# A decoder layer in float32 on one core: the second SwiGLU's gate and up blocks in seven half products, all products in 256 columns

## The chip, the core and the metric

One NeuronCore of a Trainium2 chip computes one hybrid decoder layer for 512 tokens. The metric is the time of one execution in microseconds of the device, as the median of several runs. A profiled execution gives the trace from which the rows below are taken; it is a run of its own, with its own time.

## What is computed

Three sub-layers, each with RMSNorm, a shift and a scale before it and a gate on its residual: a half-step SwiGLU, a token mixer (gated convolution and sparse attention), and a second half-step SwiGLU. The model width is 1024, the SwiGLU's inner width 2816.

```
def _swiglu(h, w_gate, w_up, w_down):
    return (jax.nn.silu(h @ w_gate) * (h @ w_up)) @ w_down
...
h = _modulate(_rmsnorm(x, g_ffn1), sh1, sc1)
x = x + MACARON_W * gt1 * _swiglu(h, w1_gate, w1_up, w1_down)
h = _modulate(_rmsnorm(x, g_mix), sh2, sc2)
x = x + gt2 * _hybrid_mixer(h, ...)
h = _modulate(_rmsnorm(x, g_ffn2), sh3, sc3)
x = x + MACARON_W * gt3 * _swiglu(h, w2_gate, w2_up, w2_down)
return _rmsnorm(x, g_final)
```

Everything is float32, and the weights arrive as float32.

## The kernel before

The residual x lies transposed in SBUF: 8 tiles (`DK`) of 128 channels by 512 tokens (`T`). To keep float32 precision at TensorE's float32r rate, every operand is split in two parts, a high one (ScalarE, ACT, copies it to float32r) and a low one (the difference, on VectorE, DVE, or GpSimd, POOL). A product then is three matrix products that add up in one PSUM bank: high x high, low activation x high weight, high activation x low weight. `mm3` issues these three for one chunk of 128 rows of the contraction, each over all columns (tokens) of its output, 512 where nothing else is said, 256 where a half of the tokens is asked for.

Weights come in units of 128 x 1024 values (512 KB) through four raw tiles (`load_unit`, on SP's queue), are split by `make_units` (ACT, line 378) and `low_part` (DVE or POOL, line 367) into one of four pairs of tiles `whi`, `wlo`, and are freed when their products are issued.

A SwiGLU (`ffn`) has 22 blocks of 128 inner columns (`FK`). The first three are made in the stage before, while the norm's halves come in (`first_group`, in halves of 256 tokens; in the first SwiGLU `first_products`, whose last six chunks go over 512). For each further block `project` makes the gate and then the up product, 8 chunks each, into two PSUM banks; `glu` takes the gate's silu (ACT), multiplies by the up product (DVE, line 612) and splits the result into `ghi` and `glo` (ACT, DVE line 619). After 11 blocks comes the first half of the down projection (`part`, 8 output tiles of 11 chunks), whose results are added to x (line 640), and after 22 the second, whose last two output tiles go in halves of 256 tokens, so that the norm behind it can begin (`residual`, line 544, squares on ACT, sums on DVE line 475). Behind the second SwiGLU stands the final norm: `final` scales the first half on DVE (line 1749), `turn` transposes the second and evicts four tiles on ACT or DVE.

The order on each engine is made by a planner while the program is built: `Plan` runs the tasks above, gives each operation a cost by the functions `c_act`, `c_tt`, `c_mm3` and so on, and issues in each step the one that can start first, ties by rank. Where an operation can run on DVE or POOL it takes the one that would end first, with a tax on POOL (`POOL_TAX`). Every engine then executes its list strictly in that order, waiting on semaphores. All products are issued at line 286, so the profile names them by their tiles: `hhi`, `hlo` (the normed input), `ghi`, `glo` (the inner activations), `whi`, `wlo` (weights), `b` (PSUM banks). `whik` is a kept weight tile at a stage's end.

## Time and profile before

| | |
|---|---|
| median of 3 runs | 1047.43 us (1046.82 to 1047.58) |
| the profiled execution | 1046.38 us, of which the span of its instructions is 1044.6 us |
| busy: PE, DVE, ACT, POOL | 1018.8, 608.8, 408.5, 60.2 us |
| granted clock of TensorE, mean over the span | 0.994 of full speed |
| read from HBM | 130.14 MB |

A row of a stretch or group gives the busy time, and how many instructions it holds. A matrix product's busy time reaches from its start to its modelled end, which lies in the next ones' time, since products are pipelined; so the sum of such times is not what a stretch takes, and the distance from one start to the next is the pace. "<-" names what ended an idle time. Stages can be told by the tiles: up to 59 us the first norm and the conditioning, 59 to 386 the first SwiGLU, then its tail and the norm, 410 to 676 the mixer with its output projection, 676 to 706 the second SwiGLU's first three blocks, 706 to 1017 the rest of it, and then the tail.

### The profile page before, as it was taken

To read this page: it belongs to the slowest core of one execution; us is meant where nothing else is said; L and a number is where in the kernel's file an instruction comes from. 1 tells how busy PE (TensorE), PEld (TensorE's weight loads), DVE (VectorE), ACT (ScalarE), POOL (GpSimd) and SP (SyncE) were. 2 spreads that over 40 slices of the span, in tenths; PEclk is the share of its full clock that TensorE was granted. 3 is DMA by queue.
4 is the path that set the end of the run, shared out by engine and by line. 5 is a ranking of instruction groups with operands and counts; after the bars stand their busy time and mean duration, and the time that the engine had idled before them with its cause. 6 is when DMAs were issued, how large, how long until landed. Compare 5 with 4: busy or idle time off the path is not lost.

```text
span 1044.6 us, 13818 instructions
## 1 busy us (share of the span) xinstructions
PE 1018.8 (98%) x5409; PEld 856.6 (82%) x5409; DVE 608.8 (58%) x1065; ACT 408.5 (39%) x719; POOL 60.2 (6%) x51
## 2 busy tenths in 40 slices
PE   7999999999999999998999999999999999999997
PEld 5778888888888889987878778998888888888887
DVE  4987559555555547499898986745333333333334
ACT  4553322222322233347868985334322123222321
POOL 0320000000000002012111110000000000000000
PEclk8999999999999999999999999999999999999999
DMA  9656554554555330433411004133333333333202
GB/s 336 258 214 231 194 202 175 198 201 170 194 201 189 135 106 16 133 113 106 158 39 29 14 20 147 43 103 122 99 101 101 94 91 98 101 101 93 91 19 81
DMA packets 40706, 133.60 MB, mean 128 GB/s; under 512 B 4704, under 2 KB 8032, under 8 KB 40000
## 3 DMA queue, kind: packets, MB, share of 16 engines
q1 hardware_dynamic: 40640, 132.71, 37.4%
q8 instruction: 42, 0.69, 0.2%
q14 instruction: 24, 0.20, 0.1%
HBM read 130.14 MB, written 2.10 MB: 127 GB/s over the span
## 4 chain that ended last, share of the span: by engine, by line
PE 84%; DVE 11%; ACT 2%; issue 1%; DMA 1%; SPq 0%; DVEq 0%; ACTq 0%
PE b L286 82%; DVE PT L1430 1%; DVE wlo L367 1%; DVE afirst L748 1%; DMA wfirst<-in_wa_dram 1%; DVE P L1347 1%; PE b L1419 1%; DVE q L1111 1%; DVE s L531 1%; ACT whi L378 0%; DVE s L1061 0%; ACT P L1351 0%; DVE swp L1064 0%; ACT P L1394 0%; DVE v L401 0%
## 5 line engine op out<-in xcount | busy, mean ns | idle before, releaser
L286 PE MATMUL b<-hhi,whi 128*128 128x512 f32 (+1 forms) x1020 | 380.3, 373 | 1.4 <-DVE pc L1270 1.3
L286 PE MATMUL b<-hlo,whi 128*128 128x512 f32 (+1 forms) x1020 | 375.3, 368 | 0.8 <-DVE hlo L537 0.4
L286 PE MATMUL b<-hhi,wlo 128*128 128x512 f32 (+1 forms) x1020 | 374.9, 368 | 0.0
L378 ACT ACTIVATE whi<-raw 128x1024 fp32r<-128x1024 f32 (+3 forms) x176 | 178.0, 1012 | 452.7 <-PE b L286 310.7
L367 DVE TENSOR_TENSOR wlo<-raw,whi 128x1024 fp32r<-128x1024 f32 (+3 forms) x158 | 186.6, 1182 | 213.1 <-ACT whi L378 211.8
L286 PEld LDWEIGHTS b<-hhi,whi 128*128 128x128 f32 x1020 | 192.8, 189 | 35.7 <-issue 3.9
L286 PEld LDWEIGHTS b<-hhi,wlo 128*128 128x128 f32 x1020 | 192.7, 189 | 31.9
L286 PEld LDWEIGHTS b<-hlo,whi 128*128 128x128 f32 x1020 | 192.9, 189 | 31.2 <-DVE hlo L537 1.3
L286 PE MATMUL b<-ghi,whi 128*128 128x512 f32 (+1 forms) x364 | 136.5, 375 | 0.0
L286 PE MATMUL b<-ghi,wlo 128*128 128x512 f32 (+1 forms) x364 | 135.7, 373 | 0.0
L286 PE MATMUL b<-glo,whi 128*128 128x512 f32 (+1 forms) x364 | 135.7, 373 | 0.0
L612 DVE TENSOR_TENSOR s<-sg,b 128x512 f32<-128x512 f32 x44 | 30.1, 687 | 101.2 <-PE b L286 95.4
L286 PEld LDWEIGHTS b<-ghi,whi 128*128 128x128 f32 x364 | 68.5, 188 | 12.8 <-issue 0.8
L286 PEld LDWEIGHTS b<-ghi,wlo 128*128 128x128 f32 x364 | 68.5, 188 | 12.0
L286 PEld LDWEIGHTS b<-glo,whi 128*128 128x128 f32 x364 | 68.6, 188 | 11.9
L879 DVE SCALAR_TENSOR_TENSOR ada<-araw,cact,ada 128x1024 f32<-128x1024 f32 x49 | 62.8, 1281 | 8.5 <-DMA araw<-in_wa_dram 8.1
L367 POOL TENSOR_TENSOR wlo<-raw,whi 128x1024 fp32r<-128x1024 f32 (+2 forms) x18 | 41.4, 2299 | 258.2 <-ACT whi L378 190.0
L544 DVE SCALAR_TENSOR_TENSOR x<-b,mod,x 128x512 f32<-128x512 f32 (+1 forms) x30 | 19.1, 642 | 38.5 <-PE b L286 38.4
L462 ACT ACTIVATE s<-x 128x256 f32<-128x256 f32 (+1 forms) x41 | 19.5, 491 | 55.1 <-DVE x L544 53.7
L535 ACT ACTIVATE hhi<-s,mod 128x256 fp32r<-128x256 f32 (+1 forms) x42 | 20.9, 534 | 32.4 <-DVE s L531 29.4
L619 DVE TENSOR_TENSOR glo<-s,ghi 128x512 fp32r<-128x512 f32 x44 | 32.2, 736 | 0.0
L1430 DVE TENSOR_TENSOR PT<-b,PT 128x384 fp32r<-128x384 f32 (+1 forms) x48 | 27.9, 594 | 4.0 <-ACT PT L1428 3.9
(241 smaller groups left out, 962.9 us busy)
## 6 DMA issues: line engine op xcount, KB each, us to landing
araw<-in_wa_dram SPq DMA_DIRECT2D x56, 512.0 KB
raw<-in_f1b_dram SPq DMA_DIRECT2D x38, 512.0 KB
raw<-in_f2b_dram SPq DMA_DIRECT2D x38, 512.0 KB
raw<-in_f1d_dram SPq DMA_DIRECT2D x22, 512.0 KB
raw<-in_f2d_dram SPq DMA_DIRECT2D x22, 512.0 KB
raw<-in_wib_dram SPq DMA_DIRECT2D x14, 512.0 KB
wfirst<-in_wa_dram SPq DMA_DIRECT2D x5, 1024.0 KB
raw<-in_wc_dram SPq DMA_DIRECT2D x8, 512.0 KB
```

What stands on the lines that cost most here:

```text
L286: nc.tensor.matmul(o, lhsT, rhs, start=start, stop=stop)
L367: (nc.vector if e == DVE else nc.gpsimd).tensor_sub(wlo_of[j][:, :n], raw_of[i][:, :n], whi_of[j][:, :n].bitcast(F32))
L378: nc.scalar.activation(whi_of[j][:, :n], raw_of[raw_at[u]][:, :n], AF.Copy)
L462: nc.scalar.activation(o[:, ts], x[d][:, ts], AF.Square)
L531: nc.vector.scalar_tensor_tensor(t, x[d][:, ts], am[:, s, d:d + 1], rb(), op0=OP.mult, op1=OP.mult)
L535: nc.scalar.activation(hhi[d][:, ts], t, AF.Identity, bias=sh)
L544: nc.vector.scalar_tensor_tensor(x[d][:, ts], bank_of[b][:, ts], gate, x[d][:, ts], op0=OP.mult, op1=OP.add)
L612: nc.vector.tensor_mul(scr_of[q], sg_of[k], bank_of[bu])
L619: nc.vector.tensor_sub(glo[j], scr_of[q], ghi[j].bitcast(F32))
L748: nc.vector.scalar_tensor_tensor(a[:, 0], w[:, k], cact[:, k:k + 1], a[:, 0], op0=OP.mult, op1=OP.add)
L879: nc.vector.scalar_tensor_tensor(a, w, cact[:, k:k + 1], a, op0=OP.mult, op1=OP.add)
L1430: nc.vector.tensor_sub(pl[:, :w], pt[:, :w], ph[:, :w].bitcast(F32))
```

## The change

Four things change. **(a)** `mm3` splits every output of 512 columns in two pieces of 256 (`HALVES`), and issues its three products for the first and then for the second; four chunks of the first plain gate block of either SwiGLU go in three pieces (`THIRDS`). **(b)** The second SwiGLU is a function of its own, `ffn2`. Blocks 3 to 6 are made as before (in pieces of 256); blocks 7 to 21 by `seven`. There the four quarters of a block's result (gate and up, each for the first and the second half of the tokens, A and B) come from seven products over half of the contraction and half of the tokens, where the plain way takes eight: the 2 x 2 scheme of Strassen and Winograd. Operands of four of the seven are sums. On the weight side `sums` makes them for each block (lines 461 to 472, in the raw tiles) and `sum_parts` splits them (ACT line 479, DVE or POOL line 481) into the tiles `wsh`, `wsl`; on the token side `build_t` makes four sums once (lines 819 to 829, tiles `thi`, `tlo`). `collect` adds the partial results up from two PSUM banks (lines 901 to 926). The even and the odd chunks of the contraction are the two halves; the weights are laid out for it (`KPOS`). **(c)** The down projection goes in four groups of 6, 6, 5 and 5 blocks, each after the first block of the next group. **(d)** The planner's costs are tables, `_MIXER` and `_LATE`, the latter for all after the first stage but the mixer; POOL's tax is 4 in the SwiGLUs. Left out below are the other cost functions, which read the tables, and the layout of the second SwiGLU's weights in HBM.

```
-    def mm3(o, w, x_, start, stop):
-
-        mm(o, w[0], x_[0], start, False)
-        mm(o, w[0], x_[1], False, False)
-        mm(o, w[1], x_[0], False, stop)
+    THIRDS = (slice(0, 176), slice(176, 344), slice(344, T))
+
+    def mm3(o, w, x_, start, stop, pieces=HALVES):
+
+        n = o.shape[-1]
+        if n != T or x_[0].shape[-1] != T:
+            pieces = (slice(0, n),)
+        for ts in pieces:
+            x0, x1 = x_[0][:, ts], x_[1][:, ts]
+            mm(o[:, ts], w[0], x0, start and ts is pieces[0], False)
+            mm(o[:, ts], w[0], x1, False, False)
+            mm(o[:, ts], w[1], x0, False, stop and ts is pieces[-1])
...
+_LATE = dict(act=(0.19, 0.85e-3), tt=(0.16, 1.04e-3), stt=(0.215, 1.04e-3), ts=(0.2, 0.54e-3), ptt=(0.2, 2.5e-3),
+             pts=(0.26, 0.83e-3), mm=0.1133, dma=0.4e-3, small=0.19)
...
 def c_mm3(n):
-    return PE, 3 * max(n / 2370, 0.105)
+    return PE, 3 * _cost["mm"] * max(n / 256, 1)
...
+    def sums(p):
...
+        x = yield scr
+        s1 = scr_of[x]
+        e = yield c_tt(T), (*c_ptt(T), W_TAX)
+        either(e).tensor_add(s1, up[:, E], up[:, O])
+        e = yield c_tt(T), (*c_ptt(T), W_TAX)
+        either(e).tensor_sub(up[:, E], ga[:, E], up[:, E])
+        done(p.third)
+        go(R_W, sum_parts(p, "1", s1, scr, x))
+        yield made[a]
+        e = yield c_tt(T), (*c_ptt(T), W_TAX)
+        either(e).tensor_sub(ga[:, E], s1, ga[:, E])
+        p.freed(scr, x, give)
+        go(R_W, sum_parts(p, "2", ga[:, E], raws, raw_at[a]))
+        e = yield c_tt(T), (*c_ptt(T), W_TAX)
+        either(e).tensor_sub(ga[:, O], ga[:, O], ga[:, E])
+        go(R_W, sum_parts(p, "4", ga[:, O], raws, raw_at[a]))
...
+            def product(o, w, x_, start=False):
+
+                yield PE, DK // 2 * 3 * 0.1133
+                for e in range(DK // 2):
+                    (w0, w1), (x0, x1) = w(e), x_(e)
+                    for i, (u, v) in enumerate(((w0, x0), (w0, x1), (w1, x0))):
+                        nc.tensor.matmul(o, u, v, start=start and not e and not i, stop=e == DK // 2 - 1 and i == 2,
+                                         skip_group_check=not start)
...
+            def collect(by):
+                Y = bank_of[by]
+                q = yield scr
+                v, w = scr_of[q][:, A], scr_of[q][:, B]
+                yield has[1]
+                yield c_act(T // 2)
+                nc.scalar.activation(v, X[:, A], AF.Copy)
+                done(has["copied"])
+                yield has[6]
+                yield c_tt(T // 2)
+                nc.vector.tensor_add(v, v, Y[:, A])
+                yield has[7]
+                yield c_tt(T // 2)
+                nc.vector.tensor_add(w, v, Y[:, B])
+                done(has["w"])
...
+                yield has[5]
+                yield c_tt(T // 2)
+                nc.vector.tensor_add(up[:, B], w, X[:, B])
+                done(has["up"])
+                yield has[4]
+                yield c_tt(T // 2)
+                nc.vector.tensor_add(up[:, A], v, Y[:, B])
+                give(banks, by)
+                yield has[3]
+                yield c_tt(T // 2)
+                nc.vector.tensor_add(X[:, B], v, X[:, B])
...
+            yield made[a]
+            yield from product(X[:, A], unit(a, 0), first(0, A), True)
+            done(has[1])
...
+            yield p.made["2"]
...
+            yield from product(Y[:, A], summed("2"), t_of(2), True)
+            done(has[6])
...
+            yield made[b]
+            yield from product(Y[:, B], unit(b, 0), t_of(3))
+            done(has[7])
+            yield p.made["1"]
+            yield from product(X[:, B], summed("1"), t_of(1))
+            done(has[5])
...
+            yield has["copied"]
+            yield from product(X[:, A], unit(a, DK // 2), first(1, A))
...
+            yield has["w"]
+            yield from product(Y[:, B], unit(b, DK // 2), t_of(4))
+            done(has[4])
...
+            yield p.made["4"]
+            yield has["up"]
+            yield from product(X[:, B], summed("4"), first(1, B))
+            done(has[3])
```

How the lists of the engines move, at three places. PE in the first SwiGLU, one and two chunks of a gate block before (`b` is the PSUM bank, then activation and weight):

```order
L286 MATMUL b1_64<-hhi4_111,whi2_98 128x512
L286 MATMUL b1_64<-hlo4_119,whi2_98 128x512
L286 MATMUL b1_64<-hhi4_111,wlo2_99 128x512
L286 MATMUL b1_64<-hhi5_112,whi2_98 128x512
L286 MATMUL b1_64<-hlo5_120,whi2_98 128x512
L286 MATMUL b1_64<-hhi5_112,wlo2_99 128x512
```

and the same number of instructions now:

```order
L323 MATMUL b7_70<-hhi4_109,whi3_99 128x256
L323 MATMUL b7_70<-hlo4_117,whi3_99 128x256
L323 MATMUL b7_70<-hhi4_109,wlo3_100 128x256
L323 MATMUL b7_70<-hhi4_109,whi3_99 128x256
L323 MATMUL b7_70<-hlo4_117,whi3_99 128x256
L323 MATMUL b7_70<-hhi4_109,wlo3_100 128x256
```

The six instructions that were two chunks are one chunk in two halves. In the whole program PE has 8451 products where it had 5271: 3336 are split in two, 24 are added by the thirds, and 15 x 12 are gone.

DVE in the second SwiGLU, in a run of gate and up blocks, before (`s` are scratch tiles, `raw` raw weights):

```order
L612 TENSOR_TENSOR s1_72<-sg0_5670,b5_68 128x512
L367 TENSOR_TENSOR wlo3_101<-raw3_92,whi3_100 128x1024
L619 TENSOR_TENSOR glo8_5667<-s1_72,ghi8_5656 128x512
L367 TENSOR_TENSOR wlo0_95<-raw0_89,whi0_94 128x1024
L612 TENSOR_TENSOR s2_73<-sg1_5671,b7_70 128x512
```

and now, most of one block's share:

```order
L905 TENSOR_TENSOR s0_71<-s0_71,b0_63 128x256
L435 TENSOR_TENSOR wlo3_100<-raw3_92,whi3_99 128x1024
L845 TENSOR_TENSOR glo1_7628<-s3_74,ghi1_7622 128x512
L908 TENSOR_TENSOR s0_71<-s0_71,b0_63 128x256
L463 TENSOR_TENSOR raw0_89<-raw1_90,raw0_89 128x512
L914 TENSOR_TENSOR s4_75<-s0_71,b6_69 128x256
L481 TENSOR_TENSOR wsl0_7645<-raw2_91,wsh0_7644 128x512
L481 TENSOR_TENSOR wsl1_7647<-raw2_91,wsh1_7646 128x512
L918 TENSOR_TENSOR s4_75<-s0_71,b0_63 128x256
L435 TENSOR_TENSOR wlo0_94<-raw1_90,whi0_93 128x1024
L922 TENSOR_TENSOR b6_69<-s0_71,b6_69 128x256
L468 TENSOR_TENSOR raw1_90<-s2_73,raw1_90 128x512
```

Collections of one block (lines 905 to 922) stand between the sums and splits of the next one's weights (lines 463 to 481); each waits in this order.

DVE at the program's end, before:

```order
L413 SCALAR_TENSOR_TENSOR v2_80<-v2_80 128x2
L415 TENSOR_TENSOR v2_80<-v2_80 128x2
L417 SCALAR_TENSOR_TENSOR v2_80<-v2_80 128x2
L1779 TENSOR_SCALAR o1_5645<-b0_63,v2_80 128x512
L1779 TENSOR_SCALAR o3_5647<-b6_69,v2_80 128x512
```

and now:

```order
L533 TENSOR_TENSOR v2_80<-v2_80 128x2
L535 SCALAR_TENSOR_TENSOR v2_80<-v2_80 128x2
L2117 SCALAR_TENSOR_TENSOR s0_71<-x_88,col_86,b1_64 128x256
L2117 SCALAR_TENSOR_TENSOR s2_73<-x_88,col_86,b1_64 128x256
L2117 SCALAR_TENSOR_TENSOR s4_75<-x_88,col_86,b1_64 128x256
L2117 SCALAR_TENSOR_TENSOR s3_74<-x_88,col_86,b1_64 128x256
```

After the second half's norm (`v`) DVE evicted two of four output tiles; now it has four of the first half's multiplications left there (`final`), and ACT evicts all four.

## Rows read from the trace of the kernel before

**Rows 1.** The page: busy shares by engine, and the chain's shares.

```profile
PE 1018.8 (98%) x5409; PEld 856.6 (82%) x5409; DVE 608.8 (58%) x1065; ACT 408.5 (39%) x719; POOL 60.2 (6%) x51
...
PE 84%; DVE 11%; ACT 2%; issue 1%; DMA 1%; SPq 0%; DVEq 0%; ACTq 0%
```

**Rows 2.** Stretches by stage: us, busy us and (instructions) by engine, clock, DMA, GB/s.

```profile
59.00:386.00 327.00, 327.00 (x1483) 266.54 (x1484) 195.51 (x209) 95.11 (x123) 8.23 (x3) 1.00 0.53 189
410.00:676.00 266.00, 257.89 (x1638) 221.80 (x1639) 219.04 (x551) 171.60 (x374) 32.28 (x24) 1.00 0.25 79
676.00:706.00 30.00, 30.00 (x252) 30.00 (x252) 14.96 (x27) 11.64 (x17) 0.00 (x0) 1.00 0.32 96
706.00:1017.00 311.00, 311.00 (x1374) 257.50 (x1373) 110.09 (x119) 88.69 (x112) 0.00 (x0) 1.00 0.30 93
```

**Rows 3.** The chain that ended last, in order of time: start us, us, what.

```profile
113.00 44.35 PE b L286 x200
...
635.89 32.42 PE b L286 x185
...
676.92 353.36 PE b L286 x1724
```

**Rows 4.** Waits of 700 to 1020 us: total us, times, longest.

```profile
ACT whi L378 <- PE b L286: 146.8, 40, 4.4
```

**Rows 5.** PE's timeline: start us, busy us, line, output and inputs, shape.

```profile
676.67 0.36 PE L286 MATMUL b<-hhi,whi 128*128 128x256 f32 x1
...
705.90 0.40 PE L286 MATMUL b<-hhi,whi 128*128 128x512 f32 x1
...
1017.37 0.28 PE L286 MATMUL b<-ghi,whi 128*128 128x256 f32 x1
1017.48 0.28 PE L286 MATMUL b<-glo,whi 128*128 128x256 f32 x1
1017.60 0.28 PE L286 MATMUL b<-ghi,wlo 128*128 128x256 f32 x1
...
1023.48 0.17 PE L286 MATMUL b<-con,ssum 128*128 128x1 f32 x1
```

**Rows 6.** PE's groups of 1017.5 to 1023.5 us, each of three kinds.

```profile
L286 PE MATMUL b<-ghi,wlo 128*128 128x256 f32 x17 | 4.8, 283 | 0.0
```

**Rows 7.** PE's groups, two of 59 to 386 us, one of 410 to 676.

```profile
L286 PE MATMUL b<-hhi,whi 128*128 128x512 f32 x316 | 124.0, 392 | 0.0
...
L286 PE MATMUL b<-ghi,whi 128*128 128x512 f32 x154 | 60.4, 392 | 0.0
...
L286 PE MATMUL b<-hhi,whi 128*128 128x512 f32 x160 | 65.5, 410 | 1.4 <-DVE pc L1270 1.3
```

**Rows 8.** DVE's groups of 700 to 1035 us: busy us, mean ns.

```profile
L367 DVE TENSOR_TENSOR wlo<-raw,whi 128x1024 fp32r<-128x1024 f32 x59 | 72.3, 1225 | 112.7 <-ACT whi L378 112.1
L612 DVE TENSOR_TENSOR s<-sg,b 128x512 f32<-128x512 f32 x22 | 15.0, 688 | 64.3 <-PE b L286 63.6 <-ACT sg L608 0.7
L619 DVE TENSOR_TENSOR glo<-s,ghi 128x512 fp32r<-128x512 f32 x22 | 15.0, 685 | 0.0
...
L1749 DVE SCALAR_TENSOR_TENSOR s<-x,col,b 128x256 f32<-128x256 f32 x8 | 3.4, 475 | 0.4 <-DMA out_dram<-s 0.4
...
L475 DVE TENSOR_TENSOR ssum<-ssum,s 128x256 f32<-128x256 f32 x2 | 0.8, 421 | 0.5 <-ACT s L462 0.5
```

**Rows 9.** POOL's groups of the whole span: the 1024-column low parts.

```profile
L367 POOL TENSOR_TENSOR wlo<-raw,whi 128x1024 fp32r<-128x1024 f32 x8 | 22.7, 2838 | 190.8 <-ACT whi L378 122.7 <-DMA s<-in_pos_dram 42.1 <-PE b L1419 13.7
```

**Rows 10.** Groups of the last evictions, on DVE and on ACT.

```profile
L1779 DVE TENSOR_SCALAR o<-b,v 128x512 f32<-128x512 f32 x2 | 1.4, 748 | 0.1
...
L1777 ACT ACTIVATE o<-b,v 128x512 f32<-128x512 f32 x2 | 1.3, 684 | 2.6 <-DVE v L417 2.6
```

More of the change, by code (lines that the diff above doesn't have):

```diff
@@ L26, with _steps @@
 FH = FK // 2
+SIZES = (6, 6, 5, 5)
+GROUP = [sum(SIZES[:i]) for i in range(len(SIZES) + 1)]
+PLAIN = 7
+def _steps():
+    for g in range(len(SIZES)):
+        for f in range(max(GROUP[g], GRP), GROUP[g + 1]):
+            yield "f", f
+            if g and f == GROUP[g]:
+                yield "d", g - 1
+    yield "d", len(SIZES) - 1
+N_S = 4
+KPOS = (0, 4, 1, 5, 2, 6, 3, 7)
 NB = T // P
@@ L77 @@
 LATER, ADA_FROM = 3, 2
-KEEP = (2, 2, 0)
+N_THIRDS = 4
+KEEP = (2, 2, 2)
 N_PT = 4
@@ L318, in ffn_units, with __init__, freed, seven_units @@
         return u + [wd[1, n] for n in range(FH)]
+    pair_of = {}
+    class Pair:
+        def __init__(self, u):
+            self.u, self.slot, self.made = u, {}, {n: Event() for n in "124"}
+            self.third, self.left = Event(), {}
+        def freed(self, slots, i, give):
+            self.left[id(slots)] = self.left.get(id(slots), 2) - 1
+            if not self.left[id(slots)]:
+                give(slots, i)
+    def seven_units(wa, wb, wd, at):
+        u = [wa[d] for d in range(DK)]
+        for what, n in _steps():
+            if what == "d":
+                u += [wd[i] for i in range(GROUP[n], GROUP[n + 1])]
+                continue
+            if n >= PLAIN:
+                pair_of[at + len(u)] = pair_of[at + len(u) + 1] = Pair(at + len(u))
+            u += [wb[n - GRP, i] for i in range(2)]
+        return u
     units = ffn_units(f1a, f1b, f1d)
@@ L365, in low_part, with half, either, sum_parts @@
         n, i, j = units[u].shape[-1], raw_at[u], w_at[u]
-        e = yield c_tt(n), (*c_ptt(n), POOL_TAX)
+        e = yield c_tt(n), (*c_ptt(n), POOL_TAX if u < DK or n_ffn <= u < n_mix else W_TAX)
         (nc.vector if e == DVE else nc.gpsimd).tensor_sub(wlo_of[j][:, :n], raw_of[i][:, :n],
                                                           whi_of[j][:, :n].bitcast(F32))
-        give(raws, i)
+        if u not in pair_of or u != pair_of[u].u:
+            give(raws, i)
         done(made[u])
+    half_of, halves_ = [], Slots()
+    def half(i):
+        t, c = divmod(i, 2)
+        return tuple(v[:, c * T:(c + 1) * T] for v in half_of[t])
+    def either(e):
+        return nc.vector if e == DVE else nc.gpsimd
+    def sums(p):
+        a, b = p.u, p.u + 1
+        yield loaded[a]
+        yield loaded[b]
+        ga, up = raw_of[raw_at[a]], raw_of[raw_at[b]]
+        E, O = slice(0, T), slice(T, 2 * T)
+        x = yield scr
[14 more added lines that the diff above has]
+        go(R_W, sum_parts(p, "4", ga[:, O], raws, raw_at[a]))
+    def sum_parts(p, n, v, slots, at):
+        p.slot[n] = yield halves_
+        hi, lo = half(p.slot[n])
+        yield c_act(T)
+        nc.scalar.activation(hi, v, AF.Copy)
+        e = yield c_tt(T), (*c_ptt(T), W_TAX)
+        either(e).tensor_sub(lo, v, hi.bitcast(F32))
+        p.freed(slots, at, give)
+        done(p.made[n])
     def make_units():
@@ L374, in make_units @@
             yield loaded[u]
+            p = pair_of.get(u)
+            if p is not None and u == p.u:
+                go(R_W, sums(p))
+            elif p is not None:
+                yield p.third
             j = yield slots_of.get(u, ws)
@@ L546, in residual, with project @@
         yield from norm.add(d, ts)
-    def project(b):
+    def project(b, n_thirds=0, kpos=range(DK)):
         u = take_unit()
@@ L654, in main @@
                 bg = yield banks
-                yield from project(bg)
+                yield from project(bg, N_THIRDS if f == GRP else 0)
                 bu = yield banks
@@ L1784, in tile_hymba_layer @@
         squared = norm.squared
-        ffn(2, gp, accs, norm, end)
+        ffn2(2, gp, accs, norm, end)
         for d in range(DK):
@@ L1804, in _ffn_layout, with _seven_layout @@
     return first, rest, dn
+def _seven_layout(wg, wu, wd):
+    first, rest, _ = _ffn_layout(wg, wu, wd)
+    rest = rest.reshape(FK - GRP, 2, P, DK, P)[:, :, :, list(np.argsort(KPOS))].reshape(FK - GRP, 2, P, DK * P)
+    dn = []
+    for g, n in enumerate(SIZES):
+        d = wd.reshape(FK, P, DK, P)[GROUP[g]:GROUP[g + 1]]
+        d = d.transpose(2, 0, 1, 3).reshape(n, 8, P, P)
+        dn.append(d.transpose(0, 2, 1, 3).reshape(n, P, 8 * P))
+    return first, rest, np.concatenate(dn)
 def _layout(i):
```

249 lines of the change are left out of this document (213 added, 36 removed).

## The prediction

> **What bounds the kernel now.** I read the page's busy shares and the chain of waits first, then the stretches by stage, then the PE timeline around a change of width, then the DVE rows of the last stage. TensorE (PE) is busy for 98% of the span and stands for 84% of the chain that ended last [rows 1]. By stage this is sharper. In the two SwiGLUs (59 to 386 us and 706 to 1017 us) PE is busy all the time at a granted clock of 1.00, that is 2.4 GHz, while DVE works 195.5 of 327 us and 110.1 of 311 us [rows 2]; the chain there is one uninterrupted run of line 286, of 353.36 us in the second SwiGLU [rows 3]. The others wait for PE: ACT's splitting of weights stood 146.8 us behind it [rows 4]. So in both SwiGLUs time is what PE needs for its list of products, and nothing else. In the token mixer (410 to 676 us) PE, DVE and ACT take turns on the chain, and PE leads only in some pieces [rows 2, 3].
>
> A busy PE is not a pace, so I take the pace from starts. From 705.90 to 1017.37 us stand the 1374 products of 512 columns of the second SwiGLU: 311.47 / 1374 = **226.7 ns** from start to start. From 1017.37 to 1023.48 us stand 51 products of 256 columns: 6.11 / 51 = **119.8 ns** [rows 5, 6]; the longer stretch of 676.67 to 705.90, 243 products (and 0.1 us for the first, which starts late), gives 120.3 [rows 5]. I take 120.0. At 2.4 GHz 512 columns are 213.3 ns and 256 columns 106.7 ns, so both rows say the same thing: columns / 2.4 GHz **plus 13.3 ns for each product**, whatever its width. Each product is one instruction with its own weight load, and PE's weight loads are as many as its products in every stretch [rows 2].
>
> **What the change does to PE.** Two things, and they pull apart.
>
> *Seven for eight.* A gate and up block was 2 x 8 x 3 = 48 products of 512 columns, 48 x 226.7 = 10.88 us. In halves it would be 96 x 120.0 = 11.52 us; in seven half products it is 84 x 120.0 = 10.08 us. The change's own cost table puts a 256-column product at 0.1133 us, which is half of the 226.7 of a 512-column one; the rows say 120.0, and I use the rows.
>
> *All products in 256 columns.* Every three products of 512 columns become six of 256. Each one split costs 2 x 120.0 - 226.7 = 13.3 ns.
>
> Now by stage. *First SwiGLU:* 38 x 24 + 154 x 3 = 1374 products, and 36 of the first group, in the stretch from 59 us [rows 7], all of them on the chain: 1410 x 13.3 ns = +18.8 us, and 12 more instructions for the thirds, +0.2. No cover exists, since PE has no idle time there [rows 2]. The 72 products of 512 columns before 59 us I cost at nothing, because DVE's sums for the conditioning vector lead there; without that cover they cost 1.0 us.
>
> *Mixer:* 160 x 3 = 480 products of 512 columns [rows 7]. The 144 of the output projection lie in the 32.42 us run of PE at 635.89 [rows 3] or just before it: +1.9. The other 336 fill gaps of the attention, where PE leads the chain about half the time; half of them is +2.2. I take +4.2, with +1.9 and +6.4 (all 480) as ends.
>
> *Second SwiGLU:* before, 311.5 us and a tail of 132 products of 256 columns, 15.8 us: 327.3. After: four plain blocks 4 x 96 x 120.0 ns = 46.1 (+0.2 for thirds), fifteen in seven 15 x 10.08 = 151.2, the down projection 22 x 8 x 3 x 2 = 1056 products = 126.7: together 324.2. **-3.1 us.** The seven half products save 15 x 1.44 = 21.6 us against halves, and the halves take 18.5 of it back here.
>
> **What the change does to the others.** Per block in seven, DVE now has five sums of 256 columns out of PSUM and SBUF (about 0.43 each, nearest row 421 ns), nine operations of 512 (0.69 each) and the low parts of two units (1.23 each) [rows 8]: 2.1 + 6.2 + 2.5 = 10.8 us, where a block had 2 x 0.69 + 2 x 1.23 = 3.8. POOL takes nine pieces of this over the fifteen blocks (a 1024-column one takes 2838 ns [rows 9]), which leaves DVE about 10.2 us a block, as much as PE's 10.08. In the longest run, five blocks in a row, the DVE's list from the first split sum of a block to the last (79 instructions) adds up to 52.8 us, PE's to 50.4. Between the runs stand down groups of 28.8 to 34.6 us of PE with some 21 us of DVE work, in which DVE gets ahead, but by little over a block: four raw slots are two blocks. Queued behind a late DVE are PE's products 6, 5 and 3 (they need the summed weights), 4 and 3 (they need a bank half read out first); each has one to three products of 1.44 us ahead of it as cover. No row of before shows such a stage. The ends are 0 (DVE always ahead, as in every row of this stage now) and 15 (one us a block); I take **+3**, near the lower end, since the excess in the lists is 2 to 3 us in a run and part of it is done ahead.
>
> The T sums (four times two additions, four differences of 256 and two splits, some 18 us of DVE) lie beside the four plain blocks, 46 us of PE, in which DVE has little else. Loads stay: two units of 512 KB in 10.08 us are 104 GB/s, and the first SwiGLU's stretch moved 189 GB/s [rows 2]. ACT gains about 2.3 us a block on a stage where it worked 88.7 of 311 us [rows 2]. SP's list has the same 22 down units in four groups.
>
> *End.* The last halves of the down projection are 60 products instead of 132, so the first half's final multiplications (475 ns [rows 8]) are not done when the second half's norm is: four are left, 1.9 us on DVE, and all four last evictions go to ACT, 4 x 0.68 = 2.7 us, where two engines shared them (2 x 0.75 on DVE, 2 x 0.68 on ACT [rows 10]). +1, between 0 and 1.5.
>
> **Sum.** +19.0 + 4.2 - 3.1 + 3 + 1 = +24.1 us on the profiled execution's 1046.38 (span 1044.6, 1.8 around it): **1070.5 us**. That execution is 1.05 us under the median of the runs, which I leave in the range. Ends of this case: 17.7 + 1.9 - 3.7 = +16 and 19.4 + 6.4 - 2.5 + 8 + 1.5 = +33: 1062 to 1079, and with the median's offset and a part of the mixer's hidden gains 1058 to 1079.
>
> **Rivals.** *DVE becomes the bound of the fifteen blocks.* DVE executes in order, and its list alternates sums for the next block's weights with collections that wait for PE. If it spends 10.8 us of work and 0.35 us of such waits on a block, the block costs 11.15 us instead of 10.08, +16 in place of the 3: 1084. It decides as soon as DVE's share of a block is over PE's 10.08. For it: the two sums above are equal within 2%. Against: the down groups between the runs.
>
> *The second half of a split product finds its weights in place and pays no fixed part* (faster). Then a split is free, 256 columns cost 113.3 ns, the mixer and first SwiGLU stay, and a seven block is 9.52 instead of 10.88: -20.4 us. DVE, at 10.2, then leads the runs and gives back some 8, the end 1: 1035. Against it: in the halves at the end of before, high and low part of an activation meet the same weights in two products running, and both still start 120 ns apart [rows 5].
>
> *The fixed part is only a few ns when products of 256 columns run for hundreds of us* (faster). With 2.7 ns, 3180 more instructions cost 8.6 us and 180 half products of columns fewer save 180 x 106.7 ns = 19.2; with waits and end +4: 1040. Against it: 30 us of 256-column products at 120.3 ns, with weight loads busy in all 30.00 us [rows 2, 5]. The Trainium skill, TensorE: Matmul & The Clock Gate, section "Back-to-back issue gap", gives such a rule: columns / 2.4 GHz + 2.5 ns, 109.2 ns for 256 and 215.8 for 512. By it the change would come out at about 1039; this case's trace has 120.0 and 226.7, so the rows decide.
>
> *The change does less than it says:* the mixer hides its products, and the gap at 256 shrinks by half in the long runs; +42 becomes +21 against -19, about 1047.
>
> **Chances.** Forecast 0.72 (1058 to 1079), DVE-bound 0.12 (1079 to 1096), weights in place 0.07, small fixed part 0.05, no difference 0.04. A measurement of this kernel can tell 0.2%, 2.1 us. Slower 0.84, same 0.04, faster 0.12. A range of 1058 to 1092 holds the first case and three quarters of the second, 0.81.
>
> **What would show it.** Right: starts 120 ns apart in the first SwiGLU where they were 226.7, its stage 19 us longer and still a pure PE run; the second SwiGLU within 10 us of its 327 us, with gaps before lines of the seven blocks of a few us in all; the mixer 2 to 6 us longer. Wrong: starts about 113 or 109 ns apart; or PE waits of over 0.7 us a block in the seven blocks, put down to DVE's summed weights or bank reads; or a granted clock under 1.00 in either SwiGLU.

## The result, and the profile after

The changed kernel takes **1033.26 us** (median of 4 runs, 1031.95 to 1040.01) where the kernel before takes 1047.12 on the same chip (4 runs, 1046.51 to 1047.58): a ratio of 0.9883, interval 0.9866 to 0.99. It is 1.2% faster; I had forecast 1070.5 us and slower, and the range of 1058 to 1092 does not hold the time. The profiled execution of the changed kernel took 1032.0 us with a span of 1030.2, against a span of 1044.6 before: 14.4 us less.

The page's busy shares and the chain's shares, where [rows 1] stood:

```profile
PE 1001.6 (97%) x8589; PEld 974.7 (95%) x8589; DVE 723.5 (70%) x1281; ACT 449.6 (44%) x789; POOL 82.2 (8%) x61
...
PE 77%; DVE 17%; ACT 3%; issue 2%; DMA 1%; SPq 0%; POOL 0%; ACTq 0%; DVEq 0%
```

PE has 3180 instructions more and is busy for 17 us less. DVE has come onto the chain: 17% where it was 11%. By stage, in the columns of [rows 2] (the first four rows answer to its four; the last two are pieces of the first SwiGLU):

```profile
59.00:388.00 329.00, 328.85 (x2893) 324.84 (x2893) 191.45 (x213) 94.45 (x124) 0.00 (x0) 1.00 0.53 189
410.00:678.00 268.00, 258.98 (x2139) 245.06 (x2140) 223.54 (x562) 172.47 (x376) 33.26 (x28) 1.00 0.25 80
678.00:706.00 28.00, 28.00 (x249) 28.00 (x248) 15.57 (x27) 11.01 (x17) 3.36 (x2) 1.00 0.31 97
706.00:1017.00 311.00, 309.55 (x2723) 308.79 (x2722) 234.45 (x346) 132.09 (x186) 29.31 (x12) 1.00 0.30 94
...
118.00:158.00 40.00, 40.00 (x342) 40.00 (x341) 21.84 (x23) 10.92 (x14) 0.00 (x0) 1.00 0.51 187
162.00:380.00 218.00, 218.00 (x1930) 215.31 (x1929) 126.96 (x141) 60.10 (x76) 0.00 (x0) 1.00 0.51 183
```

The granted clock is 1.00 in every stage, as before, and the SwiGLUs still belong to PE. The first SwiGLU, which I expected to grow by 19 us, has hardly grown. PE's timeline tells why; its columns are those of [rows 5]. First comes a piece of the first SwiGLU, then the first and one late product of the second SwiGLU's first group, then a place in the runs of seven products:

```profile
90.02 0.28 PE L323 MATMUL b<-hlo,whi 128*128 128x256 f32 x1
...
90.36 0.28 PE L323 MATMUL b<-hlo,whi 128*128 128x256 f32 x1
...
678.62 0.36 PE L323 MATMUL b<-hhi,whi 128*128 128x256 f32 x1
...
706.15 0.28 PE L323 MATMUL b<-hhi,wlo 128*128 128x256 f32 x1
...
799.95 0.28 PE L876 MATMUL b<-hhi,wlo 128*128 128x256 f32 x1
800.08 0.39 PE L876 MATMUL b<-thi,whi 128*128 128x256 f32 x1
800.31 0.28 PE L876 MATMUL b<-tlo,whi 128*128 128x256 f32 x1
```

From 90.02 to 90.36 three products take 0.34 us: **113.3 ns** each, not the 120.0 that products of 256 columns took before [rows 5, 6]. The same pace comes out of the first group of the second SwiGLU: 27.53 us from its first product to the row at 706.15 (its last), 242 steps, 113.8 each with the late start of the first, where 243 took 29.23 us before [rows 5]. It does not hold everywhere. In the stretch of 118 to 158 us the clock is 1.00 and PE is never idle, but 342 products are counted; without the three or so that the window's edges cut (one is "busy" for 280 ns), 40 us / 339 = 118 ns. Counted start by start, 371 products running from 116.2 to 159.8 us stand 117.8 ns apart. In 162 to 380 us 1930 are counted, 113.1 each. So two paces occur in one stage, with the same products, tiles and clock.

The chain, first around three seven blocks in a row and then at the program's end (start us, us, what), and the waits of PE from 700 to 1020 us:

```profile
783.90 13.61 PE b L876 x120
798.06 0.95 issue
800.96 1.20 DVE wsl L481 x2
802.50 1.13 DVE wlo L435
803.97 2.47 DVE raw L468
...
822.88 3.26 DVE wlo L435
830.20 12.52 PE b L876 x108
...
1019.68 1.26 DVE s L2117 x3
...
1024.21 1.16 ACT o L2145 x2
```

```profile
PE b L876 <- DVE s L908: 1.4, 3, 0.5
```

From 797.5 to 830.2 us the chain is DVE's almost without a break, and so it is again from 889 to 911; there DVE sets the pace, as I had feared. The price is small. What the starts in all runs of seven blocks exceed 113.3 ns by (at 799.95, 819.13, 829.40, 891.41, 910.60 and 967.24 us) adds up to 2.7 us, 1.4 of it put down to line 908.

Stage by stage, all against the spans: to the first product of the second SwiGLU 678.62 instead of 676.67, **+1.95**; its first group, up to 706.26, 27.64 instead of 29.23, **-1.6**; from there to the start of the last norm's row (1017.73, before 1034.28) 311.5 instead of 328.4, **-16.9**; the end 12.5 instead of 10.3, **+2.2**. Sum -14.4. The last norm's rows, first of the changed kernel and then of the one before:

```profile
1017.73 1.69 PE L2139 MATMUL b<-con,x 128*128 128x128 f32 x14
...
1034.28 0.49 PE L1771 MATMUL b<-con,x 128*128 128x128 f32 x3
```

### The profile page after: what moved, and what is told of

Same layout as the page of the kernel before. It is cut to its first block, busy times and chain, and to the rows that moved or that the text cites. A ratio compares the mean times of both kernels' runs of the same rounds, so it can differ in the third digit from the quotient of the medians.

```text
span 1030.2 us, 20507 instructions
## 1 busy us (share of the span) xinstructions
PE 1001.6 (97%) x8589; PEld 974.7 (95%) x8589; DVE 723.5 (70%) x1281; ACT 449.6 (44%) x789; POOL 82.2 (8%) x61
## 4 chain that ended last, share of the span: by engine, by line
PE 77%; DVE 17%; ACT 3%; issue 2%; DMA 1%; SPq 0%; POOL 0%; ACTq 0%; DVEq 0%
PE b L323 67%; PE b L876 9%; DVE wlo L435 2%; DVE PT L1797 2%; DVE P L1714 1%; DVE wsl L481 1%; DVE afirst L1113 1%; DVE raw L468 1%; DMA x<-in_xT_dram 1%; DVE q L1478 1%; DVE s L649 1%; ACT whi L496 0%; DVE glo L845 0%; PE b L1786 0%; DVE s L1428 0%
## 5 line engine op out<-in xcount | busy, mean ns | idle before, releaser
L323 PE MATMUL b<-hhi,whi 128*128 128x256 f32 x1352 | 380.3, 281 | 1.3 <-DVE pc L1637 1.3
L323 PE MATMUL b<-hlo,whi 128*128 128x256 f32 x1352 | 376.0, 278 | 1.0 <-DVE hlo L655 0.6
L323 PE MATMUL b<-hhi,wlo 128*128 128x256 f32 x1352 | 375.6, 278 | 0.5 <-POOL wlo L435 0.5
L496 ACT ACTIVATE whi<-raw 128x1024 fp32r<-128x1024 f32 (+3 forms) x174 | 176.1, 1013 | 328.4 <-issue 157.2
L323 PEld LDWEIGHTS b<-hhi,whi 128*128 128x128 f32 x1352 | 255.5, 189 | 5.8 <-issue 3.5
L323 PEld LDWEIGHTS b<-hlo,whi 128*128 128x128 f32 x1352 | 254.9, 189 | 2.0 <-DVE hlo L655 1.0
L323 PEld LDWEIGHTS b<-hhi,wlo 128*128 128x128 f32 x1352 | 254.9, 189 | 0.7 <-POOL wlo L435 0.7
L323 PE MATMUL b<-ghi,whi 128*128 128x256 f32 x640 | 177.4, 277 | 0.0
L323 PE MATMUL b<-glo,whi 128*128 128x256 f32 x640 | 176.7, 276 | 0.0
L323 PE MATMUL b<-ghi,wlo 128*128 128x256 f32 x640 | 176.7, 276 | 0.0
L323 PEld LDWEIGHTS b<-glo,whi 128*128 128x128 f32 x640 | 120.2, 188 | 0.0
L435 POOL TENSOR_TENSOR wlo<-raw,whi 128x1024 fp32r<-128x1024 f32 (+2 forms) x23 | 55.6, 2419 | 193.6 <-ACT whi L496 178.1
L662 DVE SCALAR_TENSOR_TENSOR x<-b,mod,x 128x512 f32<-128x512 f32 (+1 forms) x30 | 18.9, 643 | 28.0 <-PE b L323 28.0
```

Source lines behind the costliest of these rows:

```text
L323: nc.tensor.matmul(o, lhsT, rhs, start=start, stop=stop)
L435: (nc.vector if e == DVE else nc.gpsimd).tensor_sub(wlo_of[j][:, :n], raw_of[i][:, :n], whi_of[j][:, :n].bitcast(F32))
L496: nc.scalar.activation(whi_of[j][:, :n], raw_of[raw_at[u]][:, :n], AF.Copy)
L662: nc.vector.scalar_tensor_tensor(x[d][:, ts], bank_of[b][:, ts], gate, x[d][:, ts], op0=OP.mult, op1=OP.add)
```

## The experiments

**What was open.** Why does a product of 256 columns take 113.3 ns here and 120.0 before? Theory W is a rival of the prediction: the order of the products counts, since the two halves of a split product meet the same weights. Theory P looks at a piece of the change that neither the prediction spoke of nor the excerpt of the diff shows, nor its account of the four things that change: the padding between the tiles in SBUF, where the operands lie.

```
-    for i, n in enumerate((192, 0, 0, 0)):
-        lag(n)
+    for i in range(N_W):
         whi_of.append(const.tile([P, UNIT], F32R, name=f"whi{i}"))
         wlo_of.append(const.tile([P, UNIT], F32R, name=f"wlo{i}"))
-    lag(64)
...
+        lag(64, gp)
```

`lag(n)` places an unused tile of n bytes per partition. From the tiles' sizes and their order, the first weights tile begins before at byte 69760 of a partition and the first activation tile at 103040: 33280 apart, 130 times 256. After, the two 192 and 64 bytes ahead of them are gone: 69568 and 102784, 33216 apart. All other weight and activation tiles of the two SwiGLUs are multiples of 256 bytes from these (the new `lag(64, gp)` keeps it so for the weights in the stage's own pool). So the **distance**, the weights' address less the activations', modulo 256 bytes, is 0 before and 64 after.

| kernel | base | edit | median us (range, runs) | ratio to before, interval |
|---|---|---|---|---|
| a_whole | after | 512 columns whole, no thirds | 1042.13 (1041.22 to 1043.57, 4) | 0.9962, 0.9947 to 0.9977 |
| a_place | after | padding of before | 1067.57 (1066.87 to 1068.82, 4) | 1.0205, 1.019 to 1.022 |
| b_halves | before | every 512 in halves | 1085.82 (1085.02 to 1086.3, 4) | 1.038, 1.0363 to 1.0397 |
| b_place | before | padding of after | 1061.87 (1061.52 to 1062.12, 4) | 1.0149, 1.0134 to 1.0164 |
| b_both | before | padding of after, halves | 1056.8 (1055.68 to 1059.48, 4) | 1.0105, 1.0086 to 1.0125 |
| b_thirds | before | b_both and the thirds | 1046.06 (1044.8 to 1060.04, 10) | 1.0031, 0.9991 to 1.0071 |
| a_plain | after | no block in seven products | 1051.07 (1049.33 to 1063.79, 10) | 1.0088, 1.0046 to 1.0129 |
| a_224 | after | distance 224 | 1049.82 (1048.76 to 1050.42, 7) | 1.0027, 1.0016 to 1.0038 |
| a_nothirds | after | no thirds | 1031.92 (1028.45 to 1033.21, 4) | 0.9856, 0.9834 to 0.9879 |
| a_pool | after | no thirds, POOL's tax 1 for 4 | 1036.87 (1034.52 to 1042.18, 4) | 0.9915, 0.9883 to 0.9947 |

Each ratio is to the kernel before as it ran beside that kernel (medians of 1046.17 to 1046.88 us). Two more kernels, `pace` and `starts`, measure products alone and compute nothing of the layer.

### Is it the order or the place

**a_place**, the changed kernel with the padding of before:

```
+    lag(192)
     for i in range(N_W):
...
+    lag(64)
...
-        lag(64, gp)
...
-        lag(64, gp)
```

> The changed kernel with the old kernel's padding (192 and 64 bytes around the weight tiles, none in the stages' own pools), so that weights and tokens lie 0 modulo 512 bytes apart again; all instructions stay. P: products of 256 columns start 120.0 ns apart everywhere, about 41 us more of PE, of which a few us lie in waits that are there now: 1065 to 1073, what was predicted for the change. W, and a theory R (the thirds at a stage's start set a phase that lasts): 113.3 stays, 1032.

It took 1067.57 us, 34 us more than the changed kernel, with the same instructions. Its stretch of 720 to 1010 us, PE only (us, busy and count, clock, DMA share, GB/s):

```profile
720.00:1010.00 290.00, 290.00 (x2422) 1.00 0.32 99
```

290 us / 2419 = 119.9 ns, and no gap: the waits for DVE are gone, now that a block takes PE longer. Nothing but addresses differs, so the place decides, and theory W falls.

**b_halves** (the halves alone, at before's place):

```
-        mm(o, w[0], x_[0], start, False)
-        mm(o, w[0], x_[1], False, False)
-        mm(o, w[1], x_[0], False, stop)
+        n = o.shape[-1]
+        pieces = HALVES if n == T and x_[0].shape[-1] == T else (slice(0, n),)
+        for ts in pieces:
+            x0, x1 = x_[0][:, ts], x_[1][:, ts]
+            mm(o[:, ts], w[0], x0, start and ts is pieces[0], False)
+            mm(o[:, ts], w[0], x1, False, False)
+            mm(o[:, ts], w[1], x0, False, stop and ts is pieces[-1])
```

> The old kernel with every product of 512 columns split in two of 256, and nothing else. P: 120.0 ns apart as at its ends now; 1410 + 1374 products split and exposed cost 13.3 ns each, +37 us, and the mixer 2 to 6: about 1088. W: 113.3 ns, a split costs nothing, about 1047 or, with the halves that it has anyway at 113.3, 1042.

39.7 us more than before, 120.0 ns everywhere (2419 in the same 290 us). Here halves have the price that the prediction gave them: 3336 x 13.3 ns would be 44.4, and some of the mixer's lie beside other work.

**b_place** (before, with the padding of after, as in the diff above):

> The old kernel with the padding of the changed one, and nothing else: weights and tokens 64 bytes apart modulo 512. P: its products of 256 columns (some 840) go from 120.0 to 113.3 ns, about 5 us less, 1042; if whole products gain the same 6.7 ns, about 1021. W and R: 1047.

15.7 us more than before. The same edit that makes 256 columns faster makes 512 slower. **a_whole** shows the same from the other side:

```
-    def mm3(o, w, x_, start, stop, pieces=HALVES):
+    def mm3(o, w, x_, start, stop, pieces=(FULL,)):
...
-            mm3(bank_of[b], cols(u, kpos[d]), h_of(d), d == 0, d == DK - 1, THIRDS if d < n_thirds else HALVES)
+            mm3(bank_of[b], cols(u, kpos[d]), h_of(d), d == 0, d == DK - 1, THIRDS if d < n_thirds else (FULL,))
```

> The changed kernel with its products of 512 columns whole again (no halves, no thirds); the seven half products stay at 256 columns, and every tile stays where the changed kernel has it. Theory P (placement: the distance in SBUF between the weights and the tokens of a product, 0 modulo 512 bytes before and 64 now, sets the part of a product that is not columns): the halves in the seven blocks keep 113.3 ns; the whole products take either 226.7 ns, then the time is that of the changed kernel, about 1032 us, or they lose half of their 13.3 ns as the halves did, 220.0 ns, then it is about 1016. Theory W (width: the shorter pace comes of issuing all in 256 columns): whole products 226.7, halves back at 120.0, 1260 x 6.7 ns = 8 us more than the changed kernel, about 1041.

PE's timeline of a_whole in the first SwiGLU:

```profile
89.65 0.40 PE L323 MATMUL b<-hhi,whi 128*128 128x512 f32 x1
...
90.36 0.39 PE L323 MATMUL b<-hhi,whi 128*128 128x512 f32 x1
```

These three products take 0.71 us; the steps between whole products are of two lengths, about 231 and 236 ns, and from 62 to 386 us their mean is 233.3, while the sevens' products of 256 stay at 113.3. This is neither W's account (226.7 and 120) nor either of P's guesses for the wide ones (226.7 or 220.0): I had not thought that the place could cost the one width what it gives the other. Per 512 columns it stands 226.7 whole and 240.0 in halves at distance 0, and 233.3 whole and 226.7 in halves at distance 64.

### What of the place it is

**pace** runs streams of 96 products, each stream with its own distance between weights and activations and its own tile name (n256r64x: 256 columns, distance 64).

> Nothing of the layer: streams of 96 products in threes as the kernels have them (low and high weights and tokens), the first 22 settings with 256 columns and then the same with 512, each setting with its own distance between weights and tokens in SBUF (0 to 480 bytes in steps of 32, then the same distance at other absolute places, and 512, 576 and 1024). P: the pace is one of the distance modulo 512 alone: at 0 120.0 and 226.7 ns, at 64 113.3 (or 117.8) and 233.1, and the three other places with distance 0 or 64 and the settings 512, 576 and 1024 repeat it. If there is a distance at which 512 columns take less than 226.7 or 256 less than 113.3, a better kernel follows. W: 113.3 and 226.7 at every distance.

PE's timeline, two rows of each of four streams, with 69 steps between the two (23 rounds of the three products):

```profile
26.20 0.28 PE L48 MATMUL n256r0x<-xall,wall 128*128 128x256 f32 x1
...
34.48 0.28 PE L48 MATMUL n256r0x<-xall,wall 128*128 128x256 f32 x1
...
49.56 0.28 PE L48 MATMUL n256r64x<-xall,wall 128*128 128x256 f32 x1
...
57.38 0.28 PE L48 MATMUL n256r64x<-xall,wall 128*128 128x256 f32 x1
...
306.36 0.39 PE L48 MATMUL n512r0x<-xall,wall 128*128 128x512 f32 x1
...
322.00 0.39 PE L48 MATMUL n512r0x<-xall,wall 128*128 128x512 f32 x1
...
351.33 0.40 PE L48 MATMUL n512r64x<-xall,wall 128*128 128x512 f32 x1
...
367.43 0.39 PE L48 MATMUL n512r64x<-xall,wall 128*128 128x512 f32 x1
```

8.28 / 69 = 120.0, 7.82 / 69 = 113.3, 15.64 / 69 = 226.7 and 16.10 / 69 = 233.3 ns: the four paces of the two kernels, with nothing else on the chip. All distances, ns from start to start without each stream's first 24 steps:

| distance, bytes | 0 | 32 | 64 | 96 | 128 | 160 | 192 | 224 |
|---|---|---|---|---|---|---|---|---|
| 256 columns | 120.0 | 118.4 | 113.3 | 117.3 | 118.7 | 120.0 | 117.8 | 116.7 |
| 512 columns | 226.7 | 233.3 | 233.4 | 234.3 | 232.4 | 233.3 | 228.9 | 233.3 |

From 256 to 480 bytes the row repeats within 0.03 ns. Both tiles 128 bytes further on give what 0 gives (120.0, 226.7); weights at 128 and activations at 64, or 448 and 384, give what 64 gives (113.3, 233.4). So the distance counts and not either address, with a period of 256 bytes, as far as these settings reach. For 256 columns 0 and 160 are the worst places and 64 is the best; for 512 columns 0 is the best.

**a_224** puts the changed kernel at a distance from the middle of the table (`lag(160)` and `lag(96)` for before's 192 and 64, and `lag(224, gp)`).

> The changed kernel with other padding, so that weights and tokens lie 224 bytes apart modulo 256; nothing else. P with the table of paces: 116.7 instead of 113.3 ns, on some 6850 products of 256 columns in stretches that PE bounds, +22.8 us, of which up to 4 lie where PE waits for DVE now: 1052 to 1056. If the table of the bare streams doesn't carry over to the kernel: 1033 or 1070.

```profile
720.00:1010.00 290.00, 289.39 (x2473) 1.00 0.31 97
```

1049.82 us, with 117 ns from start to start; the table's 116.7 carries over. It came out 2 us under what I expected. Two differences show in its trace: the 371 products of 116 to 160 us, which the changed kernel runs at 117.8 ns, run at 116.7 here, and PE's waits for line 910, the counterpart of 908, are 0.5 us instead of 1.4.

### The parts of the change at the new place

**b_both** (padding of after and halves in the kernel before) should have been as fast as before, since 2 x 113.3 = 226.7.

> The old kernel with both: the padding of the changed one and every product of 512 columns split in two of 256; no seven for eight. P: 113.3 ns, so a split product takes 226.7 as whole ones do now, and the some 840 products that were halves anyway gain 6.7 ns: 1041 to 1047. What is left to the changed kernel, 9 to 14 us, is then the seven for eight: 180 products of 113.3 ns are 20.4 us of PE, less the waits and the end. W: the same. A rival N (both edits are needed for something else, and the seven for eight gives nothing): about 1033.

It was 10.4 us slower than before. Its second SwiGLU, 720 to 1010 us:

```profile
720.00:1010.00 290.00, 290.00 (x2465) 1.00 0.30 93
```

290 / 2462 = 117.8 ns, all through, at distance 64 and clock 1.00, while its first SwiGLU ran at 113.3. 3041 products x 4.44 ns = 13.5 us: the second pace, seen in after for 44 us, for a whole stage. **b_thirds** adds the thirds of the changed kernel, to see whether they set the pace:

```
-            mm3(bank_of[b], cols(u, d), h_of(d), d == 0, d == DK - 1)
+            mm3(bank_of[b], cols(u, d), h_of(d), d == 0, d == DK - 1, THIRDS if d < n_thirds else HALVES)
...
-                yield from project(bg)
+                yield from project(bg, 4 if f == GRP else 0)
```

> The old kernel with the new padding and all in 256 columns, and in addition the twelve pieces of a third at the first plain gate block of either SwiGLU. If the thirds turn a stream from the pace of 117.8 to that of 113.3: the second SwiGLU's 2748 products after them lose 4.4 ns each, 12 us under the same kernel without thirds (1057): about 1045. If the pace is set otherwise: 1057, with 117.8 after the thirds too, or 113.3 from before them.

The profiled execution has 113.3 in the second SwiGLU:

```profile
720.00:1010.00 290.00, 290.00 (x2561) 1.00 0.30 93
```

But its first group, ahead of the thirds, already runs at 113.3. And the ten times fall apart, seven of 1044.8 to 1046.5 and three of 1058.8 to 1060.0, some 13 us, about what 4.44 ns a product come to: one kernel seems to have either pace. **a_nothirds** (`N_THIRDS = 0`) asks the changed kernel the same:

> The changed kernel without the pieces of a third (24 products fewer). P: the placement sets the pace, and the thirds only choose between the two paces seen at 64 bytes, 113.3 and 117.8 ns: the second SwiGLU stays at 113.3, or turns to 117.8, which is 2700 x 4.4 ns = 12 us; 1032 to 1045. R (the thirds set the phase for all that follows): 117.8 or 120.0 throughout, over 1050.

1031.92 us, the second SwiGLU at 113.3 without any thirds. It has the lowest median, but its runs overlap with after's.

**starts** asks what chooses. In every trace so far a pace lasts as long as products of 256 columns follow each other unbroken (b_both's 3041 are one such run), and changes only behind an interruption.

> Computes nothing of the layer; writes the input as output. Streams of 96 products of 256 columns, all at distance 64, follow each other without a pause in SBUF or load; ahead of each stands another interruption of PE: nothing, one or two products of 64 to 248 columns, one to four fp32 products of 128 columns, pieces of 176 and 168 columns as in the thirds, or products of 512 columns. Theory S, that the way a stream starts chooses its pace: each stream keeps one pace from its start to its end, some are at 113.3 ns and some at 117.8, the change falls on an interruption only, and the same interruption gives the same pace when it comes again. Theory E, that something else of the kernel (another engine's access to SBUF or PSUM, a transfer, or the moment) chooses: all streams at 113.3, since no other engine works here, as the streams at distance 64 did in the kernel that measured products alone, or a pace that changes within a stream.

PE's timeline behind two and behind three of the fp32 products (L57), then PE's counts in 10 us of a stream (us, busy and count, clock, DMA share, GB/s), behind two and three, again behind two and three, and behind one and four chunks in thirds:

```profile
371.65 0.28 PE L48 MATMUL b<-xall,wall 128*128 128x256 f32 x1
...
382.61 0.28 PE L48 MATMUL b<-xall,wall 128*128 128x256 f32 x1
382.73 0.83 PE L57 MATMUL trans<-raw 128*128 128x128 f32 x6
...
383.64 0.28 PE L48 MATMUL b<-xall,wall 128*128 128x256 f32 x1
...
394.18 0.28 PE L48 MATMUL b<-xall,wall 128*128 128x256 f32 x1
```

```profile
372.00:382.00 10.00, 10.00 (x87) 1.00 0.01 2
384.00:394.00 10.00, 10.00 (x91) 1.00 0.01 2
418.50:428.50 10.00, 10.00 (x87) 1.00 0.01 2
430.50:440.50 10.00, 10.00 (x91) 1.00 0.01 2
...
501.00:511.00 10.00, 10.00 (x87) 1.00 0.01 2
516.00:526.00 10.00, 10.00 (x90) 1.00 0.01 2
```

10.96 us / 93 steps = 117.8 behind two, 10.54 / 93 = 113.3 behind three. Each stream keeps its pace from its sixth step or so to its last, and the kinds of interruption that came more than once gave the same pace each time: one or two of the fp32 products gave 117.8 all three times, three or four gave 113.3 all three times; one chunk in thirds 117.8, four chunks (as the changed kernel has them) 113.3, both twice; one or two chunks of 512 columns 117.8, three 113.3, both twice. Behind one product of 64 to 248 columns it is 113.3 in eleven cases and 117.8 in thirteen, in no order that I could read. No other engine works there, so theory E falls and S stands: **the start of a stream chooses its pace**. Each repeat also stood behind a stream at the same pace as the first time, so a part played by the stream before is not ruled out.

**a_plain** (`PLAIN = 22`) takes the seven products away and leaves everything else.

> The changed kernel with no block in seven (its bound for plain blocks set to 22): placement, halves, thirds and the four down groups stay. Theory P: its 15 blocks cost 96 products instead of 84, 180 x 113.3 ns = +20.4 us of PE, less the 4 us that PE's starts show as gaps in the seven blocks (DVE's list): 1033 + 16 = about 1049; if a pace of 117.8 falls into the second SwiGLU, as in the old kernel with both edits, up to 13 us more. N: seven for eight gives nothing: 1033.

```profile
720.00:1010.00 290.00, 290.00 (x2562) 1.00 0.30 94
```

The profiled execution took 1050.05 us, at the same 113.3 as after's 1032.0: **seven for eight is worth 18.0 us**. The list is 15 x 12 products shorter, 180 x 113.3 ns = 20.4, so 2.4 us are given back, about the 2.7 us of gaps above; a_plain has none. Here too the times form two groups, six of 1049.3 to 1051.5 and four of 1062.3 to 1063.8, so the median's interval is wide.

**a_pool** gives POOL more of the sums, to shorten DVE's list (`W_TAX = 1`, no thirds).

> The changed kernel without thirds and with POOL's tax at 1 instead of 4 in the SwiGLUs, so that POOL takes 15 more pieces of DVE's work in the whole program. If PE's 4 us of gaps in the seven blocks come of DVE's list being as long as PE's: 2 to 4 us less than the changed kernel, 1029 to 1031. If a POOL piece is late itself (2.8 us for 1024 columns against 1.2 on DVE), it takes their place: 1033 to 1037.

1036.87 us, nothing won; a_nothirds, from which it differs by the tax alone, took 1031.92. PE's waits of 700 to 1020 us:

```profile
PE b L876 <- DVE s L908: 3.8, 6, 0.7
```

3.8 us where after has 1.4. Six of DVE's 15 sums of line 468 last 2.77 to 2.81 us, each beside a low part on POOL; the other nine last 0.69. So work that POOL takes holds DVE up (more of it in the next section). Another 1.8 us of the time are the second pace, 415 steps at 117.8 from 968 to 1017 us.

## Why the prediction was wrong

- **The step that failed** is "Each one split costs 2 x 120.0 - 226.7 = 13.3 ns", with the sentence that it rests on, that rows of either width show a fixed part of 13.3 ns. Both readings were right, for distance 0. The change moves all weights and activations to distance 64, and there the fixed part is 6.7 ns for 256 columns (113.3 - 106.7) and 20.0 for 512 (233.3 - 213.3). Two halves at the new place cost what one whole product cost at the old one, 2 x 113.3 = 226.7, and the +18.8 and +4.2 of the first SwiGLU and the mixer shrink to the +1.95 measured, of which 371 x 4.45 ns = 1.65 is the stretch at the second pace. It is the sign of being wrong that I had named, starts about 113 ns apart. The padding stood in no term of my sum. A hint lay in the change itself: its cost table has 0.1133 us for a product of 256 columns, which is what the new place gives, and I set it aside for rows that hold for the old one.
- **The sum itself held for the place that it was made for**: a_place, the whole change at distance 0, took 1067.6 us against my 1070.5, with 120 ns from start to start; only the +3 for waits was not needed there. (The upper end of my range has 8 us for waits, though the text puts their end at 15; the waits reached neither.) With 113.3 for 120.0 the same working gives 0 for both first stages; 4 x 96 + 15 x 84 + 1056 = 2700 products x 113.3 = 306.0 against 327.3, -21.3; -1.6 for the 243 products of the first group; +3 and +1 as they were: -18.9. Measured were -14.4. The 4.5 between them are 1.95 ahead of the second SwiGLU; 5.5 where the +3 stood (2.7 of gaps, and about as much for 12 products of the thirds and 12 of the norm's sums beyond the 2700), 2.5 more than it; 2.2 at the end where the +1 stood, 1.2 more; less 1.1 by which my 327.3 was short of the measured 328.4.
- **The rivals.** "Weights in place" had the pace, 113.3, and a time of 1035, 1.7 us from the measured, by a mechanism that does not hold: in a_place and b_halves halves meet the same weights and cost 120.0. "Small fixed part" had the direction, but 256 columns in a stage of hundreds of us keep 120.0 at distance 0 (b_halves). Its sum was wrong too: it charges 2.7 ns for each added instruction, as if the whole products had no more, while the rows have them at 226.7; two halves of 109.4 in place of each come, by the terms of my sum, to about 1002 us instead of 1040 (an estimate). The formula set beside it, from the Trainium skill, TensorE: Matmul & The Clock Gate, section "Back-to-back issue gap", is one that the section gives for a single product by itself; for a stream of weight loads and products, which is what runs here, it gives other figures. No run here measures a product by itself. I gave these two 0.12 together, because the rows of before showed 120.0 in two places; both lay at the same distance.
- **DVE in the runs of seven.** That 2.7 us of gaps stand where I had +3 is luck. I had worked the +3 out for a PE that takes 10.08 us a block; at that pace, in a_place, PE does not wait at all, and the gaps come with the 9.5 us (84 x 113.3 ns) of the new place. Nor is DVE late for the reason that I gave, the mere length of its list:

```profile
L435 DVE TENSOR_TENSOR wlo<-raw,whi 128x1024 fp32r<-128x1024 f32 x49 | 66.1, 1349 | 31.5 <-ACT whi L496 30.7 <-PE b L323 0.8
L481 DVE TENSOR_TENSOR wsl<-raw,wsh 128x512 fp32r<-128x512 f32 x30 | 19.8, 682 | 0.1
...
L468 DVE TENSOR_TENSOR raw<-s,raw 128x512 f32<-128x512 f32 x15 | 15.9, 1059 | 0.1
```

  These are DVE's groups of 700 to 1035 us, as in [rows 8]: 1349 ns for a low part where it had 1225, 1059 for line 468 beside 682 for line 481 of the same shape. The means hide two kinds. Of the 15 sums of line 468, 12 last 0.69 us as I had taken them and three 2.56; of the 49 low parts three last 3.31 to 3.33 us and the rest 1.22. Each of the six long ones starts while POOL is at a low part and ends 0.5 to 1.1 us after it; without a POOL instruction beside it none of these operations is over 1.23 us. One of the six:

```profile
812.32 2.41 POOL L435 TENSOR_TENSOR wlo<-raw,whi 128x1024 fp32r<-128x1024 f32 x1 [6.42 <-ACT whi L496]
812.50 3.31 DVE L435 TENSOR_TENSOR wlo<-raw,whi 128x1024 fp32r<-128x1024 f32 x1
```

  So the pieces given to POOL, which I had counted as relief for DVE, made its list longer: the six long operations are 12 us over the others, and the six low parts beside them would have been 6 x 1.22 = 7.3 us on DVE. Two of the long ones are the pieces of 2.47 and 3.26 us in the chain above. The sums of line 468 overwrite a raw tile that a low part reads, so some of them may have had to wait in any case; the long low parts share no tile with POOL's. No run keeps POOL out of these blocks, so what that would give back is not shown; a_pool, with more pieces on POOL, had more waits. The rival "DVE becomes the bound" had the right place and the wrong price.
- **The end** was +1 in the sum and +2.2 in the trace; the finals on DVE (1.26 us in the chain above) and the four last evictions, all on ACT, stand there on the chain as worked out.
- **Seven for eight** was right where it counts: 18.0 us in a_plain, against my 21.6 less 3. At 113.3 ns for 120.0 the 21.6 become 20.4.

## What to carry to other kernels

A pace read from one kernel holds for the tiles' places in that kernel: before it is carried over, compare the distance of the two operands' addresses, and treat an unused tile of a few bytes in a diff as an edit with a price. Here 64 bytes are worth -6.7 ns for each product of 256 columns and +6.7 for each of 512, and 34 us in the changed kernel. Splitting products and moving tiles belong together: either alone made the kernel before slower (by 39.7 and 15.7 us), and both together, without the seven products, gained nothing (b_both 1056.8 us, b_thirds 1046.06). A helper engine's help has to be read in the trace of the engine that it helps: here DVE's operations beside POOL's low parts took 2.6 to 3.3 us instead of 0.7 to 1.2.

## What the runs showed that I had not expected

- The start-to-start time of a product depends on the distance between its weights and its activations in SBUF, with a period of 256 bytes, and not on either address: 113.3 to 120.0 ns for 256 columns, 226.7 to 234.3 for 512, with different best places (pace, in steps of 32 bytes).
- At distance 64 products of 256 columns have two lasting paces, 113.3 and 117.8 ns, at a granted clock of 1.00 and with PE never idle. What PE did right ahead of a stream chooses, and the choice holds until the next interruption, be it 11 us or 358. By which rule is open. Distance 224 has a second pace as well: in a_224 166 steps from 812.9 to 832.4 us are 117.8 ns, the others 116.7. Open too is why b_thirds has three runs of ten that are 13 us longer, and a_plain four: there is no trace of these, and that they ran at 117.8 is worked out from the times alone. The changed kernel's own 1040.01 us, 8 us over its fastest, is as open. The four chunks in thirds of the changed kernel do set 113.3 in starts; a_nothirds has it without them.
